# First modulation weights among the tokens; second key block's transposes two steps later; score tiles' PSUM banks opened in front of the gate tiles'

## The chip, the core and the metric

The kernel runs on one core of a Trainium2 chip. The metric is the device time of one execution in microseconds (us), taken as the median of several runs. The engines are PE (TensorE), ACT (ScalarE), DVE (VectorE), POOL (GpSimd) and SP (SyncE, which only issues DMAs here). PSUM has eight banks of 128 x 512 fp32 values, into which PE writes.

## What is computed

One layer over 1024 latent and 256 context tokens of width 1024 (1280 rows in all). The core of the reference, cut to what the change touches:

```python
mod_x = silu(c) @ w_ada + b_ada          # shifts, scales and gates of the latent tokens
mod_c = silu(c_ctx) @ w_ada + b_ada      # the same for the context tokens
px = modulate(rms_norm(x, norm1_w), sh1, sc1) @ w_in      # h * (1 + scale) + shift
pc = modulate(rms_norm(ctx, norm1_w), csh1, csc1) @ w_in
dn = gated_deltanet(...)        # q, k, v by a centred 5-tap convolution and SiLU; chunked, both directions
na = neighborhood_attention(...)        # 8 x 16 window keys plus all context keys
x = x + g1 * (concat(dn, na) @ w_out)
x = x + g2 * swiglu(modulate(rms_norm(x, norm2_w), sh2, sc2))
```

Products with weights are taken in split precision: an operand is kept as a high part (rounded to fp32r) and a low part (the rest), and three products hi*hi, hi*lo, lo*hi are added.

## The kernel before, in words

**Layout.** Channels lie on partitions, tokens in the free dimension. The 1024 channels of the tokens are eight tiles `xt` of 128 x 1280 (L680), and the normed and modulated tokens are eight pairs `hh` (high) and `hl` (low). A row of 1280 tokens is cut into three segments of 256 (context), 512 and 512 tokens, one PSUM bank each.

**Prologue (L674 to L778).** SP issues the eight token tiles, two raw key weights `fraw` (L684) and then eight modulation weights `wada` of 1 MB each (`load_ada`, L676), three of them ahead of the constants. The block from L732 on is scheduled by hand: PE, DVE and ACT run it in the order in which it is written. Token tiles are squared in pairs on ACT (L737, L739), the two squares are added on DVE (L740), and PE sums the result over the channels with a matrix of ones (L742), two passes for each of three segments. ACT then makes the inverse root `rs` with Ln (L744, once for each segment) and Exp (L745, once for the whole row). `first[0].prefetch` splits the first key block's weight on DVE (L201, L204), `first[1].prefetch` the second's on POOL. `ada(j)` (L701 to L708) multiplies the vectors `silu(c)` (`wide`) by the j-th modulation weight on PE (16 matmuls) and copies the row `arow` on DVE or ACT; `column(j)` (L710 to L719) turns it into columns on PE (L714) and makes `mod` and the scale `w1s` on DVE. `normed_tile(k)` (L721 to L730) makes `xt*w1s*rs` on DVE (L726), `hh` on ACT (L727) and `hl` on DVE (L729). Tile 0 of the first two key blocks is multiplied at L757 in three groups of six matmuls (whi*hh, wlo*hh, whi*hl; two blocks by three segments), with ada(1) in front of them, column(1) and tile 1's norm behind the first, ada(2) and column(2) behind the last. Tiles 1 to 7 follow in `mm_part` (L413), with the later ada steps between them by the table AHEAD.

**Jobs (from L1076).** A list of jobs follows: 0 to 3 are the four key blocks k0 to k3 (`Block`), 4 is the first half of the gate columns (`Wide`, eight tiles of 128 tokens, L609), then the neighbourhood keys and queries, the queries, values and last the second gate half. A Block's matmuls run in eight steps, one for each token tile. Its banks are then evacuated: for the first key blocks ACT copies the middle tap (L446) and DVE adds the other four straight out of PSUM (L455), later ones are copied by ACT to `cr` (L461). Then SiLU (L476) on ACT. `finish()` (L530 to L574) is a generator: for a key block three groups of transposes (4, 4 and 2 of them; L537 on PE, copied by ACT at L539), then three groups of k*k products (4, 4 and 2; L561, copied at L562), then a pass on POOL and the stores. A step of `finish()` of job n-2 is drawn at each matmul step k of job n from k = 3 on (or at each gate tile), and what is left is drawn at the end of job n. While the first gate half runs, `finish()` of the block two jobs back and then that of the block before are drawn tile by tile.

**PSUM.** Three pools follow one another: `psb` (eight banks in a ring), `psa` from a later job on (four banks `blk`, others of two), and, from the last job on, `psg` (two banks, L1105), which holds the gate tiles while the attention takes its score tiles `sc` (three banks each, two of them) from the same pool list (L295). `psa` is closed before `psg` opens.

Of the kernel before, what the change touches and what calls it, by code (L numbers as in the profile page):

```python
# [88 lines left out]
def hybrid(ctx, tc, a, dbg):  # L89
# [166 lines left out]
    psum = []  # L256

    def attention(nw):
# [33 lines left out]
        def pair(heads, bts, vw, vc, half, cb, out):  # L292

            r0 = 4 * half
            sc = psum[-1].tile([128, 1536], F32, name="sc", tag="sc", bufs=2)  # L295
# [75 lines left out]
    na, kept = [], []  # L371
# [11 lines left out]
    with ExitStack() as bs:  # L383
# [282 lines left out]
        with ExitStack() as xs:  # L666
# [11 lines left out]
            for k in range(KT):  # L678
                x = xp.tile([128, T], F32, name=f"xt{k}", tag=f"xt{k}")
                sp.dma_start(x, a["xcT"][k])  # L680
                xt.append(x)
# [3 lines left out]
            for j in range(3):  # L685
                load_ada(j)
# [34 lines left out]
            def normed_tile(k, cuts=(slice(0, CT), slice(CT, T))):  # L721
                t = xt[k]
                parts = [(x, mod1[:, k, int(x.start < CT):int(x.start < CT) + 1]) for x in cuts]
                for x, sh in parts:
                    j = int(x.start < CT)
                    dve.scalar_tensor_tensor(t[:, x], t[:, x], w1s[:, k, j:j + 1], rs[:, x], op0=OP.mult, op1=OP.mult)  # L726
                    act.activation(hh[k][:, x], t[:, x], AF.Identity, bias=sh)  # L727
                for x, sh in parts:
                    dve.scalar_tensor_tensor(hl[k][:, x], t[:, x], sh, hh[k][:, x].bitcast(F32),  # L729
                                             op0=OP.add, op1=OP.subtract)  # L730

            with tc.manual_schedule(engines={mybir.EngineType.PE, mybir.EngineType.DVE, mybir.EngineType.Activation}):  # L732
                sums = [bank() for _ in SEGS]
                segs = [slice(s0, s0 + n) for s0, n in SEGS]
                for k in range(0, KT, 2):
                    sq = [xp.tile([128, T], F32, name="sq%d" % i, tag="sq%d" % i, bufs=2 + i) for i in range(2)]
                    act.activation(sq[0], xt[k], AF.Square)  # L737
                    for s in segs if k == KT - 2 else [slice(0, T)]:
                        act.activation(sq[1][:, s], xt[k + 1][:, s], AF.Square)  # L739
                        dve.tensor_tensor(sq[1][:, s], sq[0][:, s], sq[1][:, s], OP.add)  # L740
                    for p, s in zip(sums, segs):
                        pe.matmul(p[:, :s.stop - s.start], M[C_ONE], sq[1][:, s], start=k == 0, stop=k == KT - 2)  # L742
                for p, s in zip(sums, segs):
                    act.activation(rs[:, s], p[:, :s.stop - s.start], AF.Ln, bias=b_eps, scale=1.0 / D)  # L744
                act.activation(rs, rs, AF.Exp, scale=-0.5)  # L745
                first[0].prefetch(raws[0], dve, dve)
                first[1].prefetch(raws[1], pool, pool)
                ada(0, dve.tensor_copy)
                column(0)
                normed_tile(0, segs)  # L750
                ada(1, act.copy)
                for b in first:
                    b.banks()
                for j, (w, x) in enumerate(((0, hh), (1, hh), (0, hl))):
                    for b in first:
                        for o, s in b.outs:
                            pe.matmul(o, b.w[w][:, 0], x[0][:, s], start=j == 0, stop=False)  # L757
                        if j == 0 and b is first[1]:
                            column(1)
                            normed_tile(1)  # L760
# [320 lines left out]
        bg2, tail = Background(), None  # L1081
# [7 lines left out]
        for n in range(2, len(jobs) + 2):  # L1089
# [13 lines left out]
            if final:  # L1103
                psa.close()
                psum.append(scan_psum.enter_context(tc.tile_pool(name="psg", bufs=1, space=PSUM)))  # L1105
# [5 lines left out]
            if isinstance(j, Wide):  # L1111
                for t, _ in enumerate(j.tiles()):
                    if t > 1 or not final:
                        next(fin, 0)
# [14 lines left out]
            elif j:  # L1129
                for k in range(KT):  # L1130
# [5 lines left out]
                    if k >= 3 and next(fin, 0) == 0:  # L1136
                        done.add(n - 2)
# [4 lines left out]
            for _ in fin:  # L1142
                pass
            done.add(n - 2)
# [679 lines left out]
```

## Time and profile before

| | us |
|---|---|
| median of 3 runs | 1515.09 |
| the runs | 1510.95, 1515.09, 1518.55 |
| the profiled execution's own time | 1512.36 |
| its span in the profile | 1510.6 |
| PE busy | 1462.2 (97%) |
| DVE busy | 996.8 (66%) |
| ACT busy | 703.5 (47%) |

The span is cut into rows of the timeline as follows: start, duration, engine, line, operation, what it writes and reads, its shapes, how many instructions the row holds, and in brackets the idle time of the engine before it with what ended it. A window row has the busy time of PE, PE's weight loads, DVE, ACT and POOL, the clock granted to PE as a share of full speed, the busy share of the DMA engines and GB/s. A row of waits names the engine that waits, for what and whom, total us, times and the longest. A DMA row gives the number of transfers, KB each and the median us from issue to landing. Ends of matmuls are modelled, so rows of PE that follow each other overlap a little; the distance between their starts is the pace.

### The profile page before, as it was taken

How to read it: one execution, taken by the hardware profiler on the slowest of the kernel's cores; microseconds unless marked ns; L12 is line 12 of the kernel's file. 1: busy time of each engine (PE TensorE's matmuls, PEld its weight loads, DVE VectorE, ACT ScalarE, POOL GpSimd, SP SyncE). 2: the span in 40 equal slices, each digit the busy share in tenths (PEclk: the TensorE clock that was granted, in tenths of full speed). 3: DMA queues.
4: the chain of work that ended last, by engine and by line, in shares of the span. 5: the costliest groups of instructions: out<-in, count | busy, mean ns of one | idle time of the engine just before them, and what ended most of it. 6: DMA issues, size and time to landing. Idle time of an engine off the chain costs nothing.

```text
span 1510.6 us, 23890 instructions
## 1 busy us (share of the span) xinstructions
PE 1462.2 (97%) x8702; PEld 1223.5 (81%) x8702; DVE 996.8 (66%) x1716; ACT 703.5 (47%) x1389; POOL 236.7 (16%) x286
## 2 busy tenths in 40 slices
PE   6999999999999998999999999999999999999998
PEld 3788797877788877887878888888888888888887
DVE  5773589875463745778867389766665567598652
ACT  5453442456663246656853284333333334354440
POOL 1054601456652201111210000000000000000000
PEclk9999999999999999999999999999999999999999
DMA  9274122778665569998539205433333335798742
GB/s 389 75 215 143 54 78 72 244 222 248 195 191 174 157 187 291 290 263 279 163 112 343 79 28 166 141 105 105 105 105 105 105 105 174 260 360 279 251 140 84
DMA packets 205398, 267.36 MB, mean 177 GB/s; under 512 B 15968, under 2 KB 113760, under 8 KB 204256
## 3 DMA queue, kind: packets, MB, share of 16 engines
q1 hardware_dynamic: 197680, 260.01, 53.2%
q10 hardware_dynamic: 7600, 5.81, 1.2%
q8 instruction: 69, 1.13, 0.3%
q14 instruction: 49, 0.40, 0.1%
HBM read 201.02 MB, written 68.94 MB: 179 GB/s over the span
## 4 chain that ended last, share of the span: by engine, by line
PE 51%; ACT 1%; DVE 1%; issue 0%; DMA 0%; POOL 0%; DVEq 0%; POOLq 0%; ACTq 0%
PE ps L1398 28%; PE ps L1741 14%; PE ps L1527 3%; PE ps L1375 1%; PE ps L1549 1%; PE sc L332 1%; PE sc L322 1%; PE sc L309 1%; PE ps L1252 0%; PE ps L1261 0%; DMA z<-z_d 0%; ACT sq L1302 0%; ACT bt L315 0%; DVE bt L313 0%; PE ps L223 0%
## 5 line engine op out<-in xcount | busy, mean ns | idle before, releaser
L1459 ACT CAST uhi<-wq 128x512 fp32r<-128x512 f32 x101 | 61.3, 622 | 135.9 <-issue 84.6
L413 PE MATMUL blk<-hh,whi 128*128 128x512 f32 (+1 forms) x410 | 121.0, 389 | 1.6 <-ACT kk L562 1.4
L1459 ACT CAST uhi<-ws 128x512 fp32r<-128x512 f32 x91 | 54.0, 621 | 146.3 <-PE ps L1398 91.4
L413 PE MATMUL blk<-hl,whi 128*128 128x512 f32 (+1 forms) x410 | 113.4, 370 | 0.3 <-DVE hl L729 0.3
L609 PE MATMUL blk<-zw,hh 128*128 128x256 f32 (+1 forms) x576 | 112.3, 289 | 1.0 <-ACT cr L461 1.0
L413 PE MATMUL blk<-hh,wlo 128*128 128x512 f32 (+1 forms) x410 | 112.0, 370 | 0.6 <-POOL wlo L204 0.6
L1460 DVE TENSOR_TENSOR ulo<-wq,uhi 128x512 fp32r<-128x512 f32 x101 | 67.6, 688 | 59.1 <-ACT uhi L1459 32.7
L1398 PE MATMUL ps<-hT,uhi 128*128 128x512 f32 x336 | 103.7, 390 | 0.0
L1398 PE MATMUL ps<-lT,uhi 128*128 128x512 f32 x336 | 103.4, 389 | 0.0
L1398 PE MATMUL ps<-hT,ulo 128*128 128x512 f32 x336 | 103.4, 389 | 0.0
L609 PEld LDWEIGHTS blk<-zw,hh 128*128 128x128 f32 x576 | 90.7, 189 | 4.1 <-ACT cr L461 1.4
L1398 PE MATMUL ps<-hB,uhi 128*128 128x512 f32 x288 | 89.1, 390 | 0.0
L1398 PE MATMUL ps<-lB,uhi 128*128 128x512 f32 x288 | 88.7, 389 | 0.0
L1398 PE MATMUL ps<-hB,ulo 128*128 128x512 f32 x288 | 88.7, 389 | 0.0
L413 PEld LDWEIGHTS blk<-hh,wlo 128*128 128x128 f32 x410 | 71.0, 188 | 14.8 <-POOL wlo L204 0.9
L413 PEld LDWEIGHTS blk<-hl,whi 128*128 128x128 f32 x410 | 71.2, 188 | 14.4 <-DVE hl L729 0.8
L609 PE MATMUL blk<-zw,hl 128*128 128x256 f32 (+1 forms) x288 | 81.9, 284 | 0.0
L413 PEld LDWEIGHTS blk<-hh,whi 128*128 128x128 f32 x410 | 67.6, 190 | 16.8 <-issue 3.8
L204 POOL TENSOR_TENSOR wlo<-wraw,whi 128x1024 fp32r<-128x1024 f32 x18 | 44.8, 2488 | 186.8 <-ACT whi L203 186.5
L1398 PEld LDWEIGHTS ps<-lT,uhi 128*128 128x128 f32 x336 | 63.1, 188 | 13.1
L1398 PEld LDWEIGHTS ps<-hT,ulo 128*128 128x128 f32 x336 | 63.1, 188 | 13.1
L1398 PEld LDWEIGHTS ps<-hT,uhi 128*128 128x128 f32 x336 | 62.9, 188 | 13.0
(361 smaller groups left out, 3500.7 us busy)
## 6 DMA issues: line engine op xcount, KB each, us to landing
wq<-w_fo SPq DMA_DIRECT2D x99, 256.0 KB, 4.2
wq<-w_gu SPq DMA_DIRECT2D x88, 256.0 KB, 2.9
wad<-wa SPq DMA_DIRECT2D x64, 256.0 KB, 4.3
bt<-rpb SPq DMA_DIRECT2D x64, 192.0 KB, 3.9
t_d<-g SPq DMA_DIRECT2D x22, 512.0 KB, 3.5
fr<-t_d SPq DMA_DIRECT2D x44, 256.0 KB, 4.9
f_d<-g SPq DMA_DIRECT2D x33, 256.0 KB, 2.1
fr<-f_d SPq DMA_DIRECT2D x33, 256.0 KB, 4.2
```

What stands on the lines that cost most here:

```text
L204: lo_engine.tensor_tensor(o, r, h.bitcast(F32), OP.subtract)
L309: s = pe.matmul(sc[:, u * 640 + n0:u * 640 + n1], q, ks[i], start=i == 0, stop=i == 1)
L322: pe.transpose(sc[:, u * 640 + j * 128:u * 640 + (j + 1) * 128], bt[:, j * 128:(j + 1) * 128], ident)
L332: pe.matmul(sc[u * ND:u * ND + ND, 1280:1408], vv, pt[:, j * 128:(j + 1) * 128], start=j == 0, stop=j == 4)
L413: pe.matmul(o, ww[:, k], xx[k][:, s], start=k == 0 and j == 0, stop=k == KT - 1 and j == 2)
L609: pe.matmul(p[:, :c1 - c0], x[k][:, s], ww[:, k, c0:c1], start=k == 0 and j == 0, stop=k == KT - 1 and j == 2)
L1375: pe.matmul(o, w[wi][:, k], parts[xi][k][:, s], start=k == 4 and j == 0, stop=k == 3 and j == 2)
L1398: pe.matmul(o, w[wi][:, k], x[xi][:, k], start=first and k == 0 and j == 0, stop=k == n - 1 and j == 2, skip_group_check=True)
L1459: act.copy(hi, self.raw[key])
L1460: dve.tensor_tensor(lo, self.raw[key], hi.bitcast(F32), OP.subtract)
L1527: pe.matmul(o, w[wi][:, k], parts[xi][k][:, s], start=k == 0 and j == 0, stop=k == KT - 1 and j == 2)
L1741: pe.matmul(o[b], w[wi][:, b], F[xn, p][xi], start=n in (0, 1, 5) and p == 0 and j == 0, stop=p == NFB // 2 - 1 and j == 2, skip_group_che ...
```

## The change

It has three parts. First, in the prologue: the first modulation weight is issued between token tiles 3 and 4; ada(0) and column(0) stand behind the second pair of squares; Ln and Exp are taken segment by segment, with the pieces of tile 0's `hh` between them; the matmuls of tile 0 go by segment over both blocks, ada(1) stands behind their first group and column(1) with tile 1's norm behind their second. Second, while job 3 runs, `finish()` of the second key block (job 1) is drawn from k = 5 on rather than k = 3, and what is left of it goes on among the gate tiles of job 4 (`more`). Third, a pool `psc` with the score tiles is opened in front of `psg`.

```diff
--- before.py
+++ after.py
@@ -292,7 +292,7 @@
         def pair(heads, bts, vw, vc, half, cb, out):
 
             r0 = 4 * half
-            sc = psum[-1].tile([128, 1536], F32, name="sc", tag="sc", bufs=2)
+            sc = psc.pop() if len(psc) > 1 else psc[0].tile([128, 1536], F32, name="sc", tag="sc", bufs=2)
             mx = nw.tile([128, 2, 4], F32, name="mx", tag="mx", bufs=3)
             for u, (head, w0, bt) in enumerate(zip(heads, WIN, bts)):
                 qs, kh, kl = head
@@ -368,7 +368,7 @@
         next(old)
         store(*done)
 
-    na, kept = [], []
+    na, kept, psc = [], [], []
 
     def store(out, hp, half):
 
@@ -676,13 +676,15 @@
                 sp.dma_start(w, a["wa1"][j])
 
             for k in range(KT):
+                if k == 4:
+                    load_ada(0)
                 x = xp.tile([128, T], F32, name=f"xt{k}", tag=f"xt{k}")
                 sp.dma_start(x, a["xcT"][k])
                 xt.append(x)
             raws = [xp.tile([128, KT, 128], F32, name=f"fraw{i}", tag=f"fraw{i}") for i in range(2)]
             for i in range(2):
                 sp.dma_start(raws[i], a["w_conv"][4 + i])
-            for j in range(3):
+            for j in range(1, 3):
                 load_ada(j)
             sp.dma_start(cst, a["cst"])
             sp.dma_start(masks, a["masks"])
@@ -718,21 +720,28 @@
                                       [128, 2, 2]), OP.add)
                 dve.tensor_scalar(w1s[:, j], m[:, 1], 1.0, n1w[:, j:j + 1], op0=OP.add, op1=OP.mult)
 
-            def normed_tile(k, cuts=(slice(0, CT), slice(CT, T))):
-                t = xt[k]
-                parts = [(x, mod1[:, k, int(x.start < CT):int(x.start < CT) + 1]) for x in cuts]
-                for x, sh in parts:
-                    j = int(x.start < CT)
-                    dve.scalar_tensor_tensor(t[:, x], t[:, x], w1s[:, k, j:j + 1], rs[:, x], op0=OP.mult, op1=OP.mult)
-                    act.activation(hh[k][:, x], t[:, x], AF.Identity, bias=sh)
-                for x, sh in parts:
-                    dve.scalar_tensor_tensor(hl[k][:, x], t[:, x], sh, hh[k][:, x].bitcast(F32),
-                                             op0=OP.add, op1=OP.subtract)
+            def high(k, x):
+                t, j = xt[k], int(x.start < CT)
+                dve.scalar_tensor_tensor(t[:, x], t[:, x], w1s[:, k, j:j + 1], rs[:, x], op0=OP.mult, op1=OP.mult)
+                act.activation(hh[k][:, x], t[:, x], AF.Identity, bias=mod1[:, k, j:j + 1])
+
+            def low(k, x):
+                j = int(x.start < CT)
+                dve.scalar_tensor_tensor(hl[k][:, x], xt[k][:, x], mod1[:, k, j:j + 1], hh[k][:, x].bitcast(F32),
+                                         op0=OP.add, op1=OP.subtract)
+
+            def normed_tile(k):
+                for part in (high, low):
+                    for x in (slice(0, CT), slice(CT, T)):
+                        part(k, x)
 
             with tc.manual_schedule(engines={mybir.EngineType.PE, mybir.EngineType.DVE, mybir.EngineType.Activation}):
                 sums = [bank() for _ in SEGS]
                 segs = [slice(s0, s0 + n) for s0, n in SEGS]
                 for k in range(0, KT, 2):
+                    if k == 4:
+                        ada(0, dve.tensor_copy)
+                        column(0)
                     sq = [xp.tile([128, T], F32, name="sq%d" % i, tag="sq%d" % i, bufs=2 + i) for i in range(2)]
                     act.activation(sq[0], xt[k], AF.Square)
                     for s in segs if k == KT - 2 else [slice(0, T)]:
@@ -740,24 +749,28 @@
                         dve.tensor_tensor(sq[1][:, s], sq[0][:, s], sq[1][:, s], OP.add)
                     for p, s in zip(sums, segs):
                         pe.matmul(p[:, :s.stop - s.start], M[C_ONE], sq[1][:, s], start=k == 0, stop=k == KT - 2)
-                for p, s in zip(sums, segs):
-                    act.activation(rs[:, s], p[:, :s.stop - s.start], AF.Ln, bias=b_eps, scale=1.0 / D)
-                act.activation(rs, rs, AF.Exp, scale=-0.5)
                 first[0].prefetch(raws[0], dve, dve)
                 first[1].prefetch(raws[1], pool, pool)
-                ada(0, dve.tensor_copy)
-                column(0)
-                normed_tile(0, segs)
-                ada(1, act.copy)
+                for i, (p, s) in enumerate(zip(sums, segs)):
+                    act.activation(rs[:, s], p[:, :s.stop - s.start], AF.Ln, bias=b_eps, scale=1.0 / D)
+                    act.activation(rs[:, s], rs[:, s], AF.Exp, scale=-0.5)
+                    if i:
+                        high(0, segs[i - 1])
+                high(0, segs[2])
+                for s in segs:
+                    low(0, s)
                 for b in first:
                     b.banks()
                 for j, (w, x) in enumerate(((0, hh), (1, hh), (0, hl))):
-                    for b in first:
-                        for o, s in b.outs:
+                    for i in range(len(segs)):
+                        for b in first:
+                            o, s = b.outs[i]
                             pe.matmul(o, b.w[w][:, 0], x[0][:, s], start=j == 0, stop=False)
-                        if j == 0 and b is first[1]:
-                            column(1)
-                            normed_tile(1)
+                    if j == 0:
+                        ada(1, act.copy)
+                    if j == 1:
+                        column(1)
+                        normed_tile(1)
                 ada(2, act.copy)
                 column(2)
                 for k in range(1, KT):
@@ -1078,7 +1091,7 @@
         def blk(n):
             return jobs[n] if 0 <= n < len(jobs) and isinstance(jobs[n], Block) else None
 
-        bg2, tail = Background(), None
+        bg2, tail, more = Background(), None, None
         bg2.add(modulation(adp, range(4), bank, 3, 1))
         first[0].evac()
         jobs[2].prefetch()
@@ -1102,6 +1115,9 @@
                 next(fill)
             if final:
                 psa.close()
+                psc.append(scan_psum.enter_context(tc.tile_pool(name="psc", bufs=1, space=PSUM)))
+                held_sc = psc[0].tile([128, 1536], F32, name="sc", tag="sc", bufs=2)
+                psc.append(held_sc)
                 psum.append(scan_psum.enter_context(tc.tile_pool(name="psg", bufs=1, space=PSUM)))
             if n + 1 < len(jobs):
                 jobs[n + 1].prefetch()
@@ -1110,7 +1126,10 @@
             nrm = blk(n - 1)
             if isinstance(j, Wide):
                 for t, _ in enumerate(j.tiles()):
-                    if t > 1 or not final:
+                    if more and next(more, 0) == 0:
+                        more = None
+                        done.add(n - 3)
+                    elif t > 1 or not final:
                         next(fin, 0)
                     if final and t > 4:
                         for _ in fin:
@@ -1133,15 +1152,18 @@
                         tail[0].norm()
                         tail[1].silu()
                         tail = None
-                    if k >= 3 and next(fin, 0) == 0:
+                    if k >= (5 if n == 3 else 3) and next(fin, 0) == 0:
                         done.add(n - 2)
                     bg.step(1)
                     if n > inv + 4:
                         bg2.step(1)
                 j.evac()
-            for _ in fin:
-                pass
-            done.add(n - 2)
+            if n == 3:
+                more = fin
+            else:
+                for _ in fin:
+                    pass
+                done.add(n - 2)
             if isinstance(j, Wide) and n == values:
                 vlat = nv_d[CT:].rearrange("(n r c) d -> r c n d", r=4, c=64)
                 for cb in range(4):
```

What stands on PE in the prologue; `sq` are the summed squares, `pm` the rows and columns of the modulation, `blk` the banks of the key blocks. Before:

```order
L742 MATMUL m<-sq_212,ones 128x512 x2
L742 MATMUL m<-sq_220,ones 128x256
L742 MATMUL m<-sq_220,ones 128x512 x2
L706 MATMUL pm<-wada,wide 32x256 x8
L714 MATMUL pm<-bias,arow 128x2 x2
L706 MATMUL pm<-wada,wide 32x256 x8
L757 MATMUL blk<-hh_129,whi 128x256
L757 MATMUL blk<-hh_129,whi 128x512 x2
```

And now, from the second pair of squares on:

```order
L751 MATMUL m<-sq_204,ones 128x256
L751 MATMUL m<-sq_204,ones 128x512 x2
L708 MATMUL pm<-wada,wide 32x256 x8
L716 MATMUL pm<-bias,arow 128x2 x2
L751 MATMUL m<-sq_228,ones 128x256
L751 MATMUL m<-sq_228,ones 128x512 x2
L751 MATMUL m<-sq_236,ones 128x256
L751 MATMUL m<-sq_236,ones 128x512 x2
L768 MATMUL blk<-hh_129,whi 128x256 x2
L768 MATMUL blk<-hh_129,whi 128x512 x4
L708 MATMUL pm<-wada,wide 32x256 x8
```

ada(0) and column(0) moved from behind the four sums to between the second and the third; ada(1) moved from in front of the first six matmuls of the key blocks to behind them.

On DVE the steps of ada(0) and column(0) (`arow`, `mod`, `w1s`) moved with them, ahead of the third pair's add:

```order
L749 TENSOR_TENSOR sq_204<-sq_203,sq_204 128x1280
L710 COPY arow<-pm 128x256
L718 TENSOR_TENSOR mod_99<-pm,prm 128x2x2
L721 TENSOR_SCALAR w1s<-mod_99,prm 128x2
L749 TENSOR_TENSOR sq_228<-sq_227,sq_228 128x1280
```

In before the three stood behind the last add and the first weight's split.

On ACT at the second key block (job 1, its `vt` and `kk`), the third (the first `cacc<-cacc`, its SiLU) and the fourth (`cacc<-blk,cw`, its evacuation), before:

```order
L539 COPY vt<-m 128x512 x2
L539 COPY vt<-m 128x256
L476 ACTIVATE cacc<-cacc 128x1280
L562 COPY kk<-m 128x512
L203 CAST whi<-wraw 128x1024
L562 COPY kk<-m 128x512
L446 ACTIVATE cacc<-blk,cw 128x256
L446 ACTIVATE cacc<-blk,cw 128x512 x2
L562 COPY kk<-m 128x256
L630 COPY abT<-blk 16x256
```

And now:

```order
L539 COPY vt<-m 128x512
L476 ACTIVATE cacc<-cacc 128x1280
L539 COPY vt<-m 128x512
L203 CAST whi<-wraw 128x1024
L539 COPY vt<-m 128x256
L630 COPY abT<-blk 16x256
L562 COPY kk<-m 128x512
L539 COPY vt<-m 128x512
L659 ACTIVATE zt<-blk 128x256
```

The copies of the transposes moved around the SiLU and those of the products behind the first tile of the gate job; the evacuation of the fourth block now stands behind the second gate tile.

## The prediction

> **What bounds the kernel now.** I read the page's busy shares first, then PE's list of waits, then windows and the timeline at the places that the diff touches.
>
> ```profile
> PE 1462.2 (97%) x8702; PEld 1223.5 (81%) x8702; DVE 996.8 (66%) x1716; ACT 703.5 (47%) x1389; POOL 236.7 (16%) x286
> ```
>
> PE is busy for 1462.2 of 1510.6 us. A microsecond counts only if PE starts or stops waiting, and such a shift early in the program is carried to the end, because the work behind it leaves no slack. The list of PE's waits and one long window say where it waits near the edits:
>
> ```profile
> PE m L537 <- DVE cacc L455: 1.7, 1, 1.7
> PE blk L609 <- ACT cr L461: 1.0, 1, 1.0
> 26.00:66.00 40.00, 39.17 (x265) 29.98 (x262) 27.82 (x46) 16.45 (x28) 0.00 (x0) 0.94 0.46 174
> ```
>
> The first row is the wait that the second edit (transposes later) is aimed at, 1.7 us, once. The second is at the place of the third edit (PSUM banks), 1.0 us, once. The window (length, then busy time of PE, PEld, DVE, ACT, POOL, granted clock, DMA share, GB/s) covers the first two key blocks: PE is busy 39.17 of 40 us. So the first edit (weights among tokens) is worth what it moves the beginning of PE's steady run, at token tile 1.
>
> **The first edit.** Before, eight token tiles come first, then two raw weights, then the modulation weights:
>
> ```profile
> xt<-xcT SPq DMA_DIRECT2D x8, 640.0 KB, 8.3
> wada<-wa SPq DMA_DIRECT2D x8, 1024.0 KB, 15.0
> 22.00:24.00 2.00, 1.46 (x20) 0.83 (x12) 0.42 (x1) 1.08 (x1) 1.80 (x1) 1.00 1.03 426
> 10.35 1.27 ACT L739 ACTIVATE sq<-xt 128x1280 f32<-128x1280 f32 x1 [0.17 <-DMA xt<-xcT]
> 14.79 1.49 DVE L740 TENSOR_TENSOR sq<-sq,sq 128x1280 f32<-128x1280 f32 x1 [1.65 <-ACT sq L739]
> 15.74 1.24 PE L742 MATMUL m<-sq,ones 128*128 128x512 f32 x3
> 10.59 10.46 PE L742 MATMUL m<-sq,ones 128*128 128x256 f32 x24 [10.59 <-DVE sq L740]
> 21.81 1.07 PE L706 MATMUL pm<-wada,wide 128*32 128x256 f32 x16 [0.76 <-DMA wada<-wa]
> 24.26 0.23 DVE L719 TENSOR_SCALAR w1s<-mod,prm 128x2 f32<-128x2 f32 x1
> ```
>
> At 426 GB/s, 1024 KB (1.05 MB) take 2.46 us. Token tile 3 lands at about 10.3 (ACT squares it from 10.35), so the moved weight lands at about 12.8, and tiles 4 to 7 land 2.46 us later than now. That alone delays the third pair's squares, whose add now starts at 14.79, by about 2.5 us.
>
> The order adds a longer delay: on DVE the three steps of ada(0) and column(0) now stand ahead of that add. They need PE, which is in the sums of the second pair: its last of six passes starts at 15.74, and the third pair's sums follow from 16.33, so I let PE be free at 16.2. From the first matmul of ada(0) to the end of the scale took 24.49 - 21.81 = 2.68 us. 16.2 + 2.68 = 18.9: the third add then starts at 18.9 in place of 14.79, **+4.1 us**, which includes the 2.5. The 12 passes of the last two pairs ran without a pause from 16.33 to 21.05; they now run from 20.45 to 25.2.
>
> ```profile
> 19.38 0.47 ACT L744 ACTIVATE rs<-m,bias 128x256 f32<-128x256 f32 x1 [1.19 <-PE m L742]
> 20.23 0.69 ACT L744 ACTIVATE rs<-m,bias 128x512 f32<-128x512 f32 x1 [0.38 <-PE m L742]
> 21.09 0.69 ACT L744 ACTIVATE rs<-m,bias 128x512 f32<-128x512 f32 x1 [0.17 <-PE m L742]
> 25.77 1.38 ACT L727 ACTIVATE hh<-xt,mod 128x512 fp32r<-128x512 f32 x2 [0.15 <-DVE xt L726]
> 26.09 2.98 PE L757 MATMUL blk<-hh,whi 128*128 128x256 f32 x6
> 28.87 0.85 PE L714 MATMUL pm<-bias,arow 128*128 128x2 f32 x4
> ```
>
> ACT's new chain, with an Exp estimated at its Ln (0.47 and 0.69): Ln0 from 23.5, Exp0, Ln1, Exp1 to 25.8; the first piece of hh to 26.3; Ln2 and Exp2 to 27.7; two pieces of hh at 0.69 to **29.1**, where before the last piece ended at 27.15. What the edit wins is visible here: a chain that is 4.1 us late leaves hh only 1.95 us late, because the modulation is ready. DVE's other work in front of xt hides behind Exp1:
>
> ```profile
> 17.18 1.82 DVE L740 TENSOR_TENSOR sq<-sq,sq 128x256 f32<-128x256 f32 x3 [0.91 <-ACT sq L739]
> 19.64 1.94 DVE L204 TENSOR_TENSOR wlo<-fraw,whi 128x1024 fp32r<-128x1024 f32 x1
> ```
>
> The last three adds run from 20.4 to 22.2 and the weight split (0.72 from 18.92 to 19.64, then 1.94; say 2.7) to 24.9. Without that cover (a weight that lands late) each microsecond past 25.3 would be a microsecond of A, as I call the edit's effect below.
>
> Then PE. Its pace hangs on the granted clock, the third number from a window's end:
>
> ```profile
> 24.00:26.00 2.00, 1.81 (x17) 0.59 (x16) 1.80 (x5) 0.74 (x2) 0.00 (x0) 0.53 0.95 388
> 28.00:30.00 2.00, 2.00 (x10) 1.81 (x9) 0.33 (x3) 0.00 (x0) 0.00 (x0) 0.50 1.01 418
> 30.00:32.00 2.00, 2.00 (x9) 1.66 (x9) 1.97 (x4) 0.58 (x2) 0.00 (x0) 0.77 1.03 426
> 24.22 1.94 PE L706 MATMUL pm<-wada,wide 128*32 128x256 f32 x16 [0.19 <-DMA wada<-wa]
> 29.58 2.02 PE L757 MATMUL blk<-hh,wlo 128*128 128x256 f32 x6
> 30.21 1.68 DVE L726 SCALAR_TENSOR_TENSOR xt<-xt,w1s,rs 128x256 f32<-128x256 f32 x2
> 31.43 1.34 PE L757 MATMUL blk<-hl,whi 128*128 128x256 f32 x6
> 31.93 1.15 ACT L727 ACTIVATE hh<-xt,mod 128x1024 fp32r<-128x1024 f32 x1 [0.69 <-DVE xt L726]
> 33.84 0.37 ACT L708 COPY arow<-pm 128x256 f32<-128x256 f32 x1 [0.76 <-PE pm L706]
> 34.73 0.83 PE L413 MATMUL blk<-hh,whi 128*128 128x256 f32 x3
> ```
>
> The clock fell from 1.00 in 22 to 24 to 0.53 and returned after 30. The same 16 matmuls took 1.07 us at 21.81 and 1.94 us at 24.22; six wlo matmuls went from 29.58 to 31.43 (1.85 us), six hl matmuls at the returned clock from 31.43 to about 32.7 (1.27 us). In the change the pauses of PE move with the late sums (it has little to do from 25.2 to 29.1), so I let the fall come again, some 4 us later. At half clock: the last two of the six whi matmuls hold 1024 of 2560 columns, 0.4 x 1.85 = 0.74, to 29.8; ada(1), which now stands here, 1.94 to 31.8; wlo 1.85 to 33.6. Only then comes column(1). From column(1) to xt of tile 1 took 30.21 - 28.87 = 1.34 us: xt starts at 35.0 in place of 30.21. Its hh ends 2.87 us behind (33.08 - 30.21), at 37.8; PE meanwhile does hl and ada(2), to about 36.7, so ada(2)'s row copy, now behind hh on ACT, is no longer released by PE but by hh. From that copy to the first matmul of tile 1: 34.73 - 33.84 = 0.89. So 38.7 in place of 34.73, **+4.0**. At full clock throughout, the two matmuls are 0.51, ada(1) 1.07 and wlo 1.27, in all 1.7 less: 37.0, +2.3. I take **A = +4.0**, since the nearest rows (24.22, 29.58) ran at half clock.
>
> What I chose: that ada(1) behind the whi matmuls costs its whole length. Before, it ran from 24.22 to 26.09, while PE would have waited for hh anyway; now it stands between two groups that are ready. That is why an earlier modulation does not become an earlier end.
>
> [...]
>
> **The second edit.**
>
> ```profile
> 99.07 0.44 PE L537 MATMUL m<-cst,cacc 128*128 128x128 f32 x2 [1.68 <-DVE cacc L455]
> 103.72 1.50 PE L561 MATMUL m<-cacc 128*128 128x128 f32 x12
> 104.27 0.74 DVE L455 SCALAR_TENSOR_TENSOR cacc<-blk,cw,cacc 128x512 f32<-128x512 f32 x1
> 105.11 1.27 ACT L476 ACTIVATE cacc<-cacc 128x1280 f32<-128x1280 f32 x1 [5.19 <-DVE cacc L455]
> 107.80 0.60 PE L537 MATMUL m<-cst,cacc 128*128 128x128 f32 x4
> 117.77 1.27 ACT L476 ACTIVATE cacc<-cacc 128x1280 f32<-128x1280 f32 x1 [4.92 <-DVE cacc L455]
> 126.64 0.60 PE L537 MATMUL m<-cst,cacc 128*128 128x128 f32 x4
> ```
>
> The second block's last transposes waited 1.68 us for a bank that DVE's taps were still reading. Two steps later that bank is free and the wait goes. The kk products move behind: their last six (103.72 to 104.98, 1.26 us) now come after the transposes of the third block. So PE reaches those at 107.80 - 1.68 - 1.26 = 104.86. What is late next is their input: the silu on ACT ends at 105.11 + 1.27 = 106.38, released by DVE's last tap at 105.01, and neither moves, since they follow the third block's matmuls, which end before. PE waits about 1.5 us, and the 1.26 us of products are still to be done: 106.4 + 1.26 + 0.1 for the copy behind the silu against 107.80. **B = 0.0**, between -1.7 (the old wait goes, the new one is covered) and +1.5 (both are paid: the copies queue behind the silu). Behind it the fourth block's evacuation moves behind a gate tile; its silu would end near 125.6 by my count instead of 119.04, and PE needs it at 126.64: 1 us is left, and I put nothing.
>
> **The third edit.**
>
> ```profile
> 523.47 0.39 PE L609 MATMUL blk<-zw,hh 128*128 128x256 f32 x1 [0.97 <-ACT cr L461]
> ```
>
> The first gate tile waits 0.97 us until ACT has copied the last value block out of its banks. With score tiles opened in front, the gate tile gets banks 6 and 7 in place of 0 and 1. In the built program it still waits for the last of those copies, and all instructions and waits behind it are the same. **C = 0**, between -0.97 and 0: no instruction is added, which excludes a loss.
>
> **Sum.** The profiled execution took 1512.36 us: 1512.36 + 4.0 + 0 + 0 = 1516.4. It lies 2.7 below the median 1515.09 of the runs shown; on that scale 1515.09 + 4.0 = **1519.1**, about 1519. What a measurement of this kernel can tell from no change is about 0.5%, 7.6 us: below 1507.5 or above 1522.7.
>
> **The rivals.**
>
> *The clock does not fall* in these steps: ada(1) at 1.07 as at 21.81, wlo at 1.27 as at 31.43. A = +2.3, 1515.09 + 2.3 = 1517.4. For it: the sums run 4.7 us without a pause just before. Against it: the fall at 24 came after such a run too. Chance 0.20. [...]
>
> *The waits go for good.* If the late tokens and the three DVE steps cost nothing, Ln0 stays at 19.38, and the same chain gives Exp1 at 21.7 and the last piece of hh at 25.0; from there the full-clock steps above (0.51, 1.07, 1.27, 1.34, 2.87, 0.89) reach tile 1 at 32.9, 1.8 earlier. With -1.68 and -0.97 that is -4.4, 1510.7. For it: ACT had 2.03 us of idle time ahead of hh (23.08 to 25.11). Against it: the DVE steps stand in order ahead of the add, whose time is not slack (PE's sums follow at once). That the third edit does nothing is part of the forecast. Chance 0.10.
>
> *Slower by more than the forecast:* the clock, once fallen, stays at half into tile 1 of both blocks. There PE has no other limit, so each microsecond at half clock past 38.7 costs half of it: 6.7 us more, the length of the fall before (24.2 to 30.9), are 3.4 us, A = +7.4, 1522.5. It decides from a granted clock of 0.50 beyond 39. For it: PE's pauses between 25.2 and 29.1 are longer than those that brought the fall before. Against it: from 29 on PE is busy, and 6.7 us of that were enough to bring the clock back. Chance 0.20.
>
> **How the numbers follow.** Forecast 0.50 at 1519. Its own range, with B from -1.7 to +1.5 and 3 us of scatter between medians (the three runs shown lie from 1510.95 to 1518.55), is 1514 to 1524. The rivals pull it to 1511 below and, with half of the slow rival, 1526 above: **1511 to 1526**. Faster than 1507.5 needs the second rival with a low median: 0.03. Slower than 1522.7: half of the slow rival, and a tenth of the forecast: 0.15. The rest, 0.82, is within.
>
> **What would show it.** In the changed profile: the first ada matmuls at about 16.2 and the third add near 18.9 (wrong if it starts before 17.5); Ln0 at 23.5; the last piece of hh ending at 29.1; tile 1's first matmul at 38.7 in place of 34.73, and a granted clock of about 0.5 between 28 and 34; no wait at the second block's third transposes, but one of some 1.5 us for the silu at the third block's first; the wait of about 0.97 us at the first gate tile unchanged. I am wrong on the first edit if tile 1 begins before 36, and on the second if PE's list shows neither wait.

## The result and the profile after

The changed kernel takes 1523.56 us (median of 6 runs, 1521.49 to 1528.42) against 1515.76 us of the kernel before in the same comparison (6 runs). The ratio is 1.0060, with a 95% interval of 1.0043 to 1.0078: 6.5 to 11.8 us slower. The forecast was +4.0; the sign, the place and two of three edits came out as worked out, the size of the first edit did not.

The page's busy shares after, and PE's list of waits (engine and line that wait, for what and whom: total us, times, longest):

```profile
PE 1467.5 (96%) x8702; PEld 1226.1 (81%) x8702; DVE 1000.2 (66%) x1716; ACT 704.2 (46%) x1391; POOL 235.2 (15%) x286
```

```profile
PE m L751 <- DVE sq L749: 12.4, 2, 10.5
PE blk L768 <- ACT hh L726: 2.5, 3, 1.3
PE m L537 <- ACT cacc L476: 1.5, 1, 1.5
PE blk L609 <- ACT cr L461: 1.0, 1, 1.0
```

The 1.7 us wait for DVE's taps is gone, and one of 1.5 us for the SiLU stands in its place; the 1.0 us at the first gate tile is unchanged. New are a second wait of the sums (12.4 us in 2, where 10.6 in 1 was the start of the program) and three for hh. PE's timeline of the changed prologue:

```profile
10.51 6.94 PE L751 MATMUL m<-sq,ones 128*128 128x256 f32 x12 [10.51 <-DVE sq L749]
17.38 1.07 PE L708 MATMUL pm<-wada,wide 128*32 128x256 f32 x16
21.52 6.26 PE L751 MATMUL m<-sq,ones 128*128 128x256 f32 x12 [1.91 <-DVE sq L749]
28.76 0.50 PE L768 MATMUL blk<-hh,whi 128*128 128x256 f32 x2 [0.98 <-ACT hh L726]
30.60 0.73 PE L768 MATMUL blk<-hh,whi 128*128 128x512 f32 x2 [1.35 <-ACT hh L726]
32.20 1.80 PE L708 MATMUL pm<-wada,wide 128*32 128x256 f32 x16
33.93 2.28 PE L768 MATMUL blk<-hh,wlo 128*128 128x256 f32 x6
40.70 0.83 PE L413 MATMUL blk<-hh,whi 128*128 128x256 f32 x3
```

Read it from the bottom: tile 1 starts at 40.70, before at 34.73, **+5.97 us**. Above it ada(1) takes its 1.73 us (to 33.93) of the path; above that the pieces of hh keep PE waiting three times; and the last two pairs' sums start at 21.52 behind a pause of 1.91 us and take 6.26 us. DVE, POOL and ACT beside them:

```profile
19.84 0.23 DVE L721 TENSOR_SCALAR w1s<-mod,prm 128x2 f32<-128x2 f32 x1
19.98 3.02 DVE L749 TENSOR_TENSOR sq<-sq,sq 128x1280 f32<-128x1280 f32 x4
24.48 3.25 DVE L204 TENSOR_TENSOR wlo<-fraw,whi 128x1024 fp32r<-128x1024 f32 x1
```

```profile
15.16 1.27 ACT L746 ACTIVATE sq<-xt 128x1280 f32<-128x1280 f32 x1 [2.84 <-DMA xt<-xcT]
26.10 0.47 ACT L755 ACTIVATE rs<-m,bias 128x256 f32<-128x256 f32 x1 [4.72 <-PE m L751]
30.76 0.72 ACT L726 ACTIVATE hh<-xt,mod 128x512 fp32r<-128x512 f32 x1 [0.21 <-DVE xt L725]
```

The fifth token tile is squared from 15.16, after ACT waited 2.84 us for its DMA; before, ACT had it from 11.96. The third add follows the scale `w1s` at 19.98, before at 14.79.

How far PE's later work is behind the kernel before, at three marks that stand in both programs (the fourth block's first transposes, the last job's first gate tile, the end):

| | tile 1 | transposes | gate tile | span |
|---|---|---|---|---|
| before | 34.73 | 126.64 | 523.47 | 1510.6 |
| changed | 40.70 | 132.93 | 530.59 | 1520.8 |
| difference | 5.97 | 6.29 | 7.12 | 10.2 |

The first edit gives 5.97, the second 0.3. The rest of the profiled 10.2 us comes later, where the two programs differ only in the PSUM banks of the last job; the last point of the next section but one returns to it.

### The profile page after: what moved, and what is told of

It reads as the page before. It is cut to its first block, busy times and chain, and to the rows that moved or that the text cites. A ratio compares the mean times of both kernels' runs of the same rounds, so it can differ in the third digit from the quotient of the medians.

```text
span 1520.8 us, 23891 instructions
## 1 busy us (share of the span) xinstructions
PE 1467.5 (96%) x8702; PEld 1226.1 (81%) x8702; DVE 1000.2 (66%) x1716; ACT 704.2 (46%) x1391; POOL 235.2 (15%) x286
## 4 chain that ended last, share of the span: by engine, by line
PE 51%; ACT 1%; DVE 0%; issue 0%; DVEq 0%; ACTq 0%
PE ps L1420 28%; PE ps L1763 14%; PE ps L1549 3%; PE ps L1397 1%; PE ps L1571 1%; PE sc L332 1%; PE sc L309 1%; PE sc L322 1%; PE ps L1295 0%; PE ps L1274 0%; PE ps L1283 0%; ACT sq L1324 0%; DVE bt L313 0%; PE ps L223 0%; ACT pt L325 0%; PE ps L1300 0%
```

## The experiments

My theory: the prologue makes the whole shift, by the late tokens, the DVE steps ahead of the third add, and ada(1) on the path. The rival: a part of the shift, the 4 us behind 140 us, is of the second and third edits. All times below are ratios to the kernel before, run on the same chip; "tile 1" is the start of its first matmul in the profiled execution.

**1. The first edit alone, and the other two alone.** `a_only` is the changed kernel with these lines put back (and the score tiles in the old pool):

```diff
-                    if k >= (5 if n == 3 else 3) and next(fin, 0) == 0:
+                    if k >= 3 and next(fin, 0) == 0:
...
-            if n == 3:
-                more = fin
```

> The first edit alone. Theory 1 (the prologue makes the shift): tile 1's first matmul stays near 40.7 as in the changed kernel (34.73 before), give or take 1.5 us for where the clock's windows fall, and the time is 6 to 8 us over the kernel before. Theory 2 (the other two edits, or what follows them, make the part of the shift behind 140 us): tile 1 again near 40.7, but the time only some 3 us over the kernel before.

`bc_only` is the kernel before with those lines and the pool `psc` put in.

> The second and third edits without the first. Theory 1: tile 1 at 34.7, give or take 1.5 us; PE's sequence 0 to 0.5 us late behind the third block's transposes, the 1.68 us wait replaced by one of about 1.5 us for the SiLU; the time within 2 us of the kernel before. Theory 2: 3 to 5 us slower, with the loss behind 250 us.

`a_only` has the ratio 1.0046 (1.0030 to 1.0061), `bc_only` 0.9993 (0.9981 to 1.0005). Tile 1 and the place of the second edit, in `a_only` and then in `bc_only`:

```profile
40.85 0.82 PE L413 MATMUL blk<-hh,whi 128*128 128x256 f32 x3
132.59 0.60 PE L537 MATMUL m<-cst,cacc 128*128 128x128 f32 x4
```

```profile
33.36 0.83 PE L413 MATMUL blk<-hh,whi 128*128 128x256 f32 x3
104.00 0.66 PE L537 MATMUL m<-cst,cacc 128*128 128x128 f32 x4 [0.22 <-ACT cacc L476]
125.31 0.66 PE L537 MATMUL m<-cst,cacc 128*128 128x128 f32 x4 [0.27 <-ACT cacc L476]
```

The first edit carries the change and the other two are worth nothing that a time can tell: the rival falls. `a_only` is 5.95 late at the fourth block's transposes, the changed kernel 6.29, so the second edit costs some 0.3 there. `bc_only` shows something else: its prologue is that of before, yet tile 1 starts at 33.36 and not at 34.73. The difference is the clock:

```profile
20.68:24.10 3.42, 2.05 (x21) 1.00 1.00 417
24.10:27.51 3.41, 3.29 (x19) 0.50 1.03 417
27.51:30.92 3.41, 3.41 (x12) 0.50 1.01 419
```

```profile
22.62:26.04 3.42, 2.31 (x33) 1.00 0.98 403
26.04:29.45 3.41, 2.74 (x13) 1.00 1.04 425
```

These are windows of the kernel before, then of `bc_only` (length, PE's busy time, granted clock, DMA share, GB/s). In both, the clock reads 1.00 or 0.50 over whole windows of 3.41 us, and the grid of these windows lies elsewhere in each execution (edges at 24.10 and at 26.04). In the kernel before, a window with 2.05 us of work ended at 24.10 and the clock fell behind it; the less busy of these two of `bc_only` had 2.31 and it did not. So the same prologue costs 1.4 us more or less by luck.

**2. The order and the weight apart.** `order_only` is `a_only` with the weight back at its place on SP's queue and ada(0) back behind the sums; `weight_only` is the kernel before with the DMA moved:

```diff
             for k in range(KT):
+                if k == 4:
+                    load_ada(0)
...
-            for j in range(3):
+            for j in range(1, 3):
                 load_ada(j)
```

> The first edit's order (Ln and Exp by segment, matmuls by segment, ada(1) behind the first six) with the weight and ada(0) at their old places. If the order costs by itself: last piece of hh ends at 28.4 (27.15 before), ada(1) no longer beside hh, tile 1 at 36.4 to 38.1, about +2.5 us. If only the early weight costs: tile 1 at 34.7 or before, 0.

> Only the DMA of the first weight moved between tiles 3 and 4; all engines in the order of before. If the tokens' delay costs by itself: third add at 18.0 in place of 14.79, sums end near 24, tile 1 about 3.3 us late (37 to 38.7). If the tokens have slack and only the new order costs: tile 1 at 34.7, or earlier, since ada(0) no longer waits for its weight.

`order_only`: 1.0023 (1.0009 to 1.0036), tile 1 at 37.62, +2.89. `weight_only`: 1.0009 (0.9999 to 1.0019), tile 1 at 38.05, +3.32. First a row of `order_only`, then two of `weight_only`:

```profile
37.62 0.87 PE L413 MATMUL blk<-hh,whi 128*128 128x256 f32 x3
```

```profile
17.80 1.49 DVE L742 TENSOR_TENSOR sq<-sq,sq 128x1280 f32<-128x1280 f32 x1 [4.29 <-ACT sq L741]
38.05 0.83 PE L413 MATMUL blk<-hh,whi 128*128 128x256 f32 x3
```

In the profile each half costs by itself; in the time only `order_only` does, since the interval of `weight_only` just reaches no change. 2.89 + 3.32 = 6.2 is about the whole, but how well that fits is partly chance: the clock fell in both runs, but at other places (0.50 from 24.62 to 31.45 in `order_only`, from 28.61 to 35.44 in `weight_only`), and experiment 1 puts the luck of the clock at 1.4 us. In `weight_only` the third add at 17.80 in place of 14.79 (14.50 to 15.24 in the other runs whose weight passes no token) is the tokens' delay without any DVE step in front of it: about 3 us. In `order_only` the last piece of hh ends at 28.85 (27.15 before): ACT takes Ln2 and Exp2 only behind the first piece of hh, and for that it waited 3.68 us for xt, because the modulation was late. ada(1) then stands on the path as in the changed kernel.

**3. ada(1) back in front.** `a_ada1_front` is `a_only` with

```diff
+                ada(1, act.copy)
                 for b in first:
                     b.banks()
...
-                    if j == 0:
-                        ada(1, act.copy)
```

> The first edit alone, but with ada(1) in front of tile 0's matmuls again, where PE waits for hh (the changed kernel's PE stood still for 0.98, 1.35 and 0.20 us there, and ada(1) behind the first six took 1.73 us of its path). If ada(1)'s place costs its whole length: tile 1 about 1.7 us earlier than 40.7, near 39.0. If the wait for hh and the clock set the end anyway: 40.7, within 0.5.

Tile 1 at 39.18, 1.67 us earlier than `a_only`; 1.0027 (1.0014 to 1.0040):

```profile
27.64 1.07 PE L708 MATMUL pm<-wada,wide 128*32 128x256 f32 x16
28.78 0.51 PE L769 MATMUL blk<-hh,whi 128*128 128x256 f32 x2
39.18 0.83 PE L413 MATMUL blk<-hh,whi 128*128 128x256 f32 x3
```

The 16 matmuls end just as the first piece of hh comes. Its place behind the first six cost its whole length.

**4. The DVE steps behind the third add.** `a_col0_late` is `a_only` with

```diff
-                    if k == 4:
-                        ada(0, dve.tensor_copy)
-                        column(0)
...
                         dve.tensor_tensor(sq[1][:, s], sq[0][:, s], sq[1][:, s], OP.add)
+                    if k == 4:
+                        ada(0, act.copy)
+                        column(0)
```

> The first edit alone, but ada(0)'s row copied by ACT behind the third pair's squares and column(0)'s DVE steps behind the third add, so that the add no longer waits for them. If the DVE chain costs more than the late tokens: the third add starts at 18.0 in place of 19.98, PE's sums of the third pair at 19.6 in place of 21.5, tile 1 near 38.7; near 37.2 if PE's shorter pause also keeps its clock up in the sums. If the late tokens are all of it: the add at 19.5 or later, tile 1 at 40.7.

This missed: tile 1 at 40.06, only 0.79 earlier; 1.0048 (1.0033 to 1.0064). The add started at 17.38 and the sums ended 4 us earlier, but PE then waited 3.90 us for hh:

```profile
24.37 3.22 DVE L725 SCALAR_TENSOR_TENSOR xt<-xt,w1s,rs 128x256 f32<-128x256 f32 x2
23.45 3.20 POOL L204 TENSOR_TENSOR wlo<-fraw,whi 128x1024 fp32r<-128x1024 f32 x1
27.52 0.50 PE L768 MATMUL blk<-hh,whi 128*128 128x256 f32 x2 [3.90 <-ACT hh L726]
40.06 0.84 PE L413 MATMUL blk<-hh,whi 128*128 128x256 f32 x3
```

Two pieces of xt took 3.22 us on DVE in place of 1.15, and POOL's `wlo` of the second block ran from 23.45 to 26.65. That gave a new theory: DVE stands still while POOL's `wlo` runs. `a_col0_lo_dve` takes POOL's `wlo` away:

```diff
-                first[1].prefetch(raws[1], pool, pool)
...
                 high(0, segs[2])
+                first[1].prefetch(raws[1], dve, pool)
```

> As a_col0_late, but the low part of the second key block's weight is made by DVE behind tile 0's xt instead of by POOL (POOL keeps the high part). In a_col0_late two pieces of xt took 3.22 us on DVE, 1.15 elsewhere, and ended when POOL's low part ended. If POOL and DVE block each other: the two pieces near 1.2 us, the last piece of hh at 28.5 in place of 30.25, tile 1 near 38.3 in place of 40.06. If something else stretched them: 3.2 us again, tile 1 at 40 or later by the low part's own time.

It held in the profile: 1.14 us for the two pieces, tile 1 at 38.09. The time, 1.0045 (1.0026 to 1.0064) from five runs, doesn't show the 2 us.

```profile
25.12 1.14 DVE L725 SCALAR_TENSOR_TENSOR xt<-xt,w1s,rs 128x256 f32<-128x256 f32 x2
38.09 0.84 PE L413 MATMUL blk<-hh,whi 128*128 128x256 f32 x3
```

Beside POOL's `wlo` the two pieces took 3.22 us, without it 1.14. How POOL holds them these runs don't show.

**5. All of it together.** `a_best` adds ada(1) in front to `a_col0_lo_dve`.

> a_col0_lo_dve with ada(1) in front of tile 0's matmuls as well: all that was found to cost beside the early weight itself is taken away. If the early weight's delay of the tokens is what remains: tile 1 at 35.0 to 36.5, still 0.3 us or more behind the kernel before (34.73), time 0 to 2 us over it. If the early weight does pay once its side costs are gone: tile 1 below 33.4.

1.0013 (0.9996 to 1.0029), tile 1 at 36.59, just past the range expected, and 1.86 us behind the kernel before:

```profile
36.59 0.84 PE L413 MATMUL blk<-hh,whi 128*128 128x256 f32 x3
```

So 40.85 - 36.59 = 4.3 us of the first edit were side costs that could be mended, and 1.9 us stay. The early weight is their likely source, but it isn't isolated here: the third add came at 17.03 (14.79 before) and ended at 18.52, yet PE began the last two pairs' sums only at 19.72, behind ada(0) and column(0), and the luck of the clock (1.4 us in experiment 1) is in this difference too.

**6. The clock.** `a_warm` (from `a_only`) and `before_warm` fill PE's pauses with matmuls of ones into PSUM columns that nobody reads; they add work and take none away:

```diff
+            def warm(p, n):
+                for _ in range(n):
+                    pe.matmul(p, ones, ones, start=True, stop=True)
...
+                warm(sums[0][:, :128], 18)
                 for k in range(0, KT, 2):
```

> The first edit alone, with 28 further 128 x 128 matmuls of ones into PSUM columns that nobody reads: 18 ahead of the first sums, 5 behind column(0), 2 behind the last sums, 3 behind the first piece of tile 0. They only fill PE's pauses. If the clock's falls, brought by those pauses, are part of the loss: granted clock 1.00 from about 8 us to 45, the last 12 sum passes in 4.4 us (6.3 before), tile 1 at 37 to 38.5. If the clock follows something else: halves in the windows again and tile 1 at 40.7, or later by the added matmuls.

> The kernel before with the same filling: 18 matmuls of ones ahead of the sums, 2 ahead of ada(0), 1 ahead of column(0). If pauses bring the fall of the clock: no half windows between 15 and 45 us and tile 1 at 33.4, as in the run of the second and third edits alone, in place of 34.73; the time 0 to 2 us under the kernel before. If not: a fall again near 24 and tile 1 at 34.7.

`a_warm`: 1.0056 (1.0034 to 1.0078), tile 1 at 38.33. `before_warm`: 0.9999 (0.9984 to 1.0015), tile 1 at 32.75. First `a_warm`, then `before_warm`:

```profile
20.77 4.56 PE L760 MATMUL m<-sq,ones 128*128 128x256 f32 x12 [0.69 <-DVE sq L758]
27.98 0.51 PE L778 MATMUL blk<-hh,whi 128*128 128x256 f32 x2 [2.20 <-ACT hh L733]
38.33 0.83 PE L413 MATMUL blk<-hh,whi 128*128 128x256 f32 x3
```

```profile
32.75 0.84 PE L413 MATMUL blk<-hh,whi 128*128 128x256 f32 x3
```

With the pauses filled the last 12 passes take 4.56 us in place of 6.26, and neither kernel's clock falls between 14 and 35 us. Both gain 2 to 2.5 us in the prologue (40.85 to 38.33, 34.73 to 32.75), so in these prologues the falls come with the pauses. Without any fall from 14 us on the kernels are still 38.33 - 32.75 = 5.6 us apart, so the falls don't make the whole difference. How much of it they make, this pair doesn't show, since `a_warm` has a new cost, the blocking of experiment 4: DVE's `wlo`, beside POOL's, ran until 26.99, and ACT waited 1.56 us for xt.

```profile
27.42 0.51 ACT L733 ACTIVATE hh<-xt,mod 128x256 fp32r<-128x256 f32 x1 [1.56 <-DVE xt L732]
```

In the changed kernel, whose sums ended later, that wait was hidden. Without it the two would be about 4 us apart by my estimate (5.6 - 1.56). A gain of 2 us in the profile of `before_warm` is below what its time can show.

**7. A weight that passes no token.** `weight_last` is `before_warm` with

```diff
+            load_ada(0)
             for i in range(2):
                 sp.dma_start(raws[i], a["w_conv"][4 + i])
...
+                ada(0, act.copy)
                 act.activation(rs, rs, AF.Exp, scale=-0.5)
```

> The kernel before with PE's pauses filled, as in before_warm, and the first weight moved to behind the last token tile and ahead of the two raw weights, its row copied by ACT in front of Exp. If the weight can come earlier as long as it passes no token: sums unchanged (Ln0 near 19), ada(0) at about 21 in place of 21.5, tile 1 near 32.1 in place of 32.75; time 1 to 3 us under the kernel before. If the raw weights, now later, take its place on the path: tile 1 at 32.75 or later.

Tile 1 at 36.49, later than both bounds of the expectation; 1.0011 (0.9993 to 1.0030).

```profile
23.96 2.07 DVE L731 TENSOR_SCALAR w1s<-mod,prm 128x2 f32<-128x2 f32 x1
23.65 2.36 POOL L204 TENSOR_TENSOR wlo<-fraw,whi 128x1024 fp32r<-128x1024 f32 x1
36.49 0.82 PE L413 MATMUL blk<-hh,whi 128*128 128x256 f32 x3
```

The raw weights came later, as feared, and with them POOL's `wlo`: an instruction on 128 x 2 values (0.23 us elsewhere) stood from 23.96 until POOL's end at 26.01. It is the same blocking again, 1.8 us on the path (xt could start at 26.1 in place of 24.3 in `before_warm`). The other 1.9 us of the 3.7 us by which tile 1 is behind `before_warm` came with a fall of the clock that `before_warm` doesn't have; it stood at 0.50 from 26.01 to 32.84:

```profile
26.01:29.43 3.42, 1.92 (x4) 0.50 1.06 427
```

So whether a weight that passes no token could pay stays open; this version also moves the raw weights. No version tried beats the time of the kernel before.

## Why the prediction was right and wrong

**The third edit: right.** No wait went, none came: 0.97 us at the first gate tile in both.

```profile
530.59 0.39 PE L609 MATMUL blk<-zw,hh 128*128 128x256 f32 x1 [0.97 <-ACT cr L461]
```

**The second edit: right**, in the changed kernel term by term. The wait of 1.68 us became one of 1.48 for the SiLU (1.5 forecast), and the sum is +0.3 in the place of 0.0.

```profile
112.58 0.66 PE L537 MATMUL m<-cst,cacc 128*128 128x128 f32 x4 [1.48 <-ACT cacc L476]
```

`bc_only` reached nearly the same sum by other terms. Its SiLU started 1.1 us earlier, counted from tile 1, and PE waited only 0.22 us for it (1.5 expected); waits of 0.28 and 0.27 us followed, and the fourth block's transposes came 0.04 us later, counted from tile 1, than before. Why that SiLU was earlier stays open.

At the fourth block I had counted on 1 us of slack. There was 0.1: the SiLU ended at 132.82 and PE's transposes started at 132.93; in `bc_only` PE waited 0.27 us there.

```profile
131.55 1.27 ACT L476 ACTIVATE cacc<-cacc 128x1280 f32<-128x1280 f32 x1 [1.04 <-DVE cacc L455]
```

**The first edit: right in mechanism, too small in size.** Tokens late, the third add behind the DVE steps, ada(1) at its whole length, column(1) behind it: each was named, and experiments 2 to 4 show the first three, the DVE steps at the sums more than at tile 1. I had +4.0 at tile 1 and it was +5.97. The term that was mis-sized is the chain up to Ln0, put at +4.1 and measured at 26.10 - 19.38 = +6.7. Two parts:

- ada(0) started at 17.38, not at 16.2, and the third add followed at 19.98, not 18.9: 1.1 us. The late tokens are not the cause here. Tile 3 did come to ACT 0.7 us later than before (11.05 against 10.35), but PE's first 12 passes ran from 10.51 to 17.4 without a pause, and in `a_only`, where tile 3 came at 10.11, ada(0) started no earlier (17.44). Some 0.4 us is a misreading: I had the second pair's sums end at 16.2 and the third's follow from 16.33. At 16.33 a weight load starts; the third pair's matmuls start at 16.60 in the kernel before:

```profile
16.60 0.59 PE L742 MATMUL m<-sq,ones 128*128 128x256 f32 x2
```

  The other 0.8 us is the pace of PE's first passes, which doubles on the way. Those of 512 columns start 0.85 us apart up to 13.31 in the kernel before, but up to 14.94 in the changed kernel, and 0.43 us apart behind that. The granted clock reads 1.00 over these stretches in both, so what sets that pace isn't shown.
- I put the fall of the clock behind the sums, into PE's wait for hh. It came into them as well:

```profile
18.75:22.16 3.41, 1.25 (x7) 1.00 1.04 423
22.16:25.57 3.41, 3.41 (x6) 0.50 1.00 416
28.99:32.40 3.41, 1.86 (x10) 1.00 1.01 418
32.40:35.81 3.41, 3.41 (x22) 0.50 1.02 423
```

The pause behind column(0) left PE 1.25 us of work in a window, and the next window, full of sums, ran at 0.50: 6.26 us in place of the 4.7 that I had used. That is 1.5 us. The pieces of hh took off 0.2 again (last piece 31.48 in place of 29.1 forecast: +2.4, of +2.6 at Ln0), and the steps behind, the half clock of ada(1) and the wlo group among them, came within 0.4 of the forecast.

None of the rivals came: the clock fell, no wait went for good, and the clock didn't stay at half into tile 1 (it reads 1.00 from 35.81 to 60).

The rows at half clock were the right ground for A. The windows ahead of the two falls in the changed kernel held 1.25 and 1.86 us of work, the one ahead of the fall in the kernel before 2.05. That the clock's edges lie 3.41 us apart I had not used. With it a fall in the sums would have been a case to price, though not a certain one, since the edges lie elsewhere in each execution.

**A cover that nearly failed.** I let DVE's split of the first raw weight take 2.7 us and hide behind Exp1. It took 4.8 (22.92 to 27.73), beside POOL's. It was still hidden, since the sums were late too; where they ended earlier it became the path (`a_warm`, experiment 6), and in `a_col0_late` POOL held the pieces of xt themselves. In the forecast I had taken DVE's durations from rows without asking what POOL did beside them.

**What stays open.** The median, 1523.56, lies in the range that I gave, 1511 to 1526, but of its +7.8 us the prologue and the second edit explain 6.3; that the rest fitted in is owed to the width of the range and to no term of the sum. The interval of +6.5 to +11.8 us begins just above 6.3, and the prologue of before varies by 1.4 us by itself. The profiled execution lost 3.9 us more behind 140 us, in places where its clock was at half and that of before was not:

```profile
580.00:630.00 50.00, 46.14 (x419) 41.19 (x419) 31.02 (x95) 31.16 (x84) 6.53 (x15) 0.93 0.84 265
```

In the kernel before the same window reads 1.00 for the clock. `a_ada1_front`, with a prologue 4.45 us late, reached its end 4.5 us late: nothing was added behind. So this part differs between executions. Over the 54 runs of the kernel before that were taken with experiments 1 to 4 and 6, without `a_col0_lo_dve`, a line of time against mean granted clock has a slope of 1.2 us for each 0.001; they average 0.9950, the changed kernel's six 0.9925, `a_only`'s eight 0.9938. That would be 3.0 and 1.4 us. Whether the later prologue brings more falls on average, or six runs happened to have them, these runs don't settle.

## What to carry to other kernels

The transfer that was moved ahead of four others on SP's queue delayed each of them by 3.0 us in `weight_only` (ACT squared tile 4 from 14.98 in place of 11.96, tile 7 from 19.74 in place of 16.74), where its own length is 2.46 us at the forecast's 426 GB/s. The steps that were moved ahead on DVE held up the third add behind them (it followed `w1s` at 19.98): an early result is worth nothing if what it passes is on the path. Before a step is put between two groups of the busy engine, ask in which pause it stood; ada(1) filled a wait for nothing and then cost 1.7 us. Compare profiled executions at marks in the middle of the program, not by their spans, since the clock's falls behind differ between executions.

## What the hardware showed

In these traces the granted clock reads 1.00 or 0.50 and changes at edges 3.41 us apart, on a grid that starts elsewhere in each execution (an edge at 24.10 in the kernel before, at 22.16 in the changed one, at 26.01 in `weight_last`). In the prologues of these runs it fell behind windows in which PE was busy 0.50 us (`a_col0_late`) to 2.13 us (`weight_last`) of the 3.41, with pauses of as little as 0.76 us in one piece (the kernel before, ahead of 21.81), and never behind more. PE's busy time alone doesn't decide: windows with 1.48 to 2.14 us of sums or of ones went by without a fall in six of the runs (`bc_only`, `a_warm`, `before_warm`, `a_col0_lo_dve`, `a_best`, `weight_last`), and one of 2.02 us with an ada step in `a_warm` (the 16 ada matmuls from 40.27 took 1.07 us, as at 1.00), while 1.82 to 1.88 us of the key blocks' matmuls were followed by a fall in three (`a_ada1_front`, `a_col0_lo_dve`, `a_best`). What decides stays open.

In two places on the path a DVE instruction that started beside POOL's `wlo` came to its end only behind it. In `a_col0_late` the two pieces of xt took 3.22 us in place of 1.15, and hh followed the first at 26.96, POOL's `wlo` having run until 26.65. In `weight_last` `w1s` took 2.07 us in place of 0.23, until 26.03, and POOL's `wlo` ran until 26.01. Not every step beside it was held: ada(0)'s row copy took 0.42 us at 22.94 in the kernel before, where POOL's `wlo` ran from 20.58 to 23.81, and the same 0.42 at 18.52 in the changed kernel, where POOL stood idle. What makes the difference isn't shown.
